# Where a decoder step makes its output weights' Strassen factors: in rooms of their own in the sample phase, one job later, some stores by ScalarE's queue

## The chip, the cores and the metric

One core of one Trainium2 chip runs the whole program. The metric is the device time of one execution in microseconds (us); the time of a kernel is the median of its runs.

## The reference, cut to what matters

One layer of a decoder is computed for 1024 prompt tokens and 64 sample tokens (1088 columns in all). Three branches (retention, causal pooling, sparse attention) are projected to the model width, gated, summed and projected once more:

```
b_a = (silu(rg) * o_a) @ w_br_a          # first branch:  (1024, D)
b_b = (silu(pg) * o_b) @ w_br_b          # second branch: (512, D)
b_c = (silu(ng) * o_c) @ w_br_c          # third branch:  (512, D)
gates = sigmoid(mg).reshape(n, t, 3, D)  # mg = rms_norm(x) @ w_in[:, 5912:]
merged = gates[:, :, 0] * b_a + gates[:, :, 1] * b_b + gates[:, :, 2] * b_c
y = rms_norm(x + merged @ w_out, final_gain)
```

Every float32 weight is split into a high and a low float16 part, and a product is three float16 matmuls. The large products (the gates, `w_br_a`, `w_out`) are made by a Strassen scheme with seven products in place of eight, so their weights are first added and subtracted by quarters and then split.

## The kernel before, in words

The program runs in phases: keys and values, prompt attention, retention, **sample phase** (pooling and the attention of the sample tokens), **output**. Within a phase the order of the instructions on each engine is set by the compiler's scheduler, from the dependences and from which buffers (rooms) are free; each engine, and each queue of DMA issues (SP's, ScalarE's, GpSimd's), works through its own list in order.

The weight pipe is a pool with rooms that all phases share: three for raw weights (`raw`, 128x1024 float32), three for high parts (`whi`) and three for low parts (`wlo`); every third one comes from a second pool (`wtile`, L212). A weight is loaded into a raw room; `wsplit` (L218) makes the high part on ScalarE (L220) and the low part on VectorE (L221).

**Sample phase.** `sample_attention` (L1020) takes the eight sequences in four groups of two. For each group SP issues two transposing DMAs of the keys (`sks<-skd`, L1041), TensorE makes the scores (L1055, L1058), VectorE and ScalarE the softmax (L1062 to L1081), TensorE transposes the weights (`ta`, `tb`, L1084 to L1087), ScalarE and VectorE split them (`sph`, `spl`, L1091 to L1094), TensorE multiplies them with the values (`so`, L1103, L1106) and transposes the sum (`sto`, L1112). The pooling branch fills TensorE beside this: its projections (`pj`, L307 to L309) and its small products (`y`, L1461) end in `gb`, the second branch's input. At its end `out_weights` (L1496) prepares `w_out` in four jobs: a job loads two row blocks of `w_out`, splits them and stores the parts to DRAM (`wod`), makes four differences on VectorE (L1517), and splits and stores these too (`wtd`). That is two loads, four splits, four differences and eight stores a job; rooms from the weight pipe, all DMAs by SP.

**Output.** For each of four pairs of column blocks the second branch's product is made: `load_c` loads and splits a pair's `w_br_b` (two halves, L231), and 96 matmuls (`pb`, L1645 to L1647) follow in eight tiles, each copied out by ScalarE (L1696). Beside each pair, `store_pair` (L1521) loads two raw rooms of `w_br_a` (L1481), has GpSimd make the Strassen sums (four operations, L1485, L1486), splits seven blocks into rooms of the weight pipe and stores them to DRAM (`wad`, L1524), all DMAs by SP. TensorE's next work is the first of eight gate jobs (`strassen`, L1551), whose left factors `load_pair` makes in the same way from `w_in`. In its first job the products "11" and "12" need raw columns only; the third, "S2", needs GpSimd's sums. The last four pairs read the stored `wad` back (`stored_pair`), and `out_rows` multiplies with `wod` and `wtd`.

Rooms that the change uses: `q` (six rooms of 128x576 float32, L1542) and `T4a` (128x4352 float16, first read in the fifth gate job).

Of the kernel before, what the change touches and what calls it, by code (L numbers as in the profile page):

```python
# [20 lines left out]
P = 128  # L21
# [106 lines left out]
class Kern:  # L128
# [32 lines left out]
    def run(self):  # L161
# [26 lines left out]
        with ExitStack() as eo:  # L188
            self.smc = self.pool(eo, "smc")
            self.pjb = R_PJ  # L190
            with ExitStack() as es:
                self.psb, ppj, psa = [self.pool(es, x, bufs=1, space=PSUM) for x in ("rpsb", "rppj", "rpsa")]
                self.retention(es, ppj, psa, right)
            self.gbp = self.pool(right, "gbp", side="right")
            self.gb = self.gbp.tile([P, 4, NG, 2, 32], F16, tag="gb", name="gb", bufs=1)
            with ExitStack() as es:
                psb, ps, pst = [self.pool(es, x, bufs=1, space=PSUM) for x in ("spsb", "sppj", "spst")]
                sp = self.pool(es, "smp", bufs=1)
                pool = self.pooling(es, ps, pst)
                next(pool)  # L200
                with self.behind():
                    self.sample_attention(sp, psb, pst)
                next(pool, None)
                self.out_weights()
# [1265 lines left out]
    def load_pair(self, wq, src, c0, c1):  # L1470
# [6 lines left out]
        for c in (c0, c1):  # L1477
# [3 lines left out]
            self.loaded = self.wq.dma_start(raw[-1].rearrange("p (k c) -> p k c", c=P),  # L1481
# [7 lines left out]
        for i, a in (("11", a11), ("12", a12), ("S2", s2), ("S1", s1), ("S3", a21), ("S4", a11), ("22", a22)):  # L1489
            if i == "S2":  # L1490
                sub(a11, a12, s2)
            t = self.wblock(wq)
# [3 lines left out]
    def out_weights(self):  # L1496

        nc = self.nc
        self.wod = self.dr.tile([P, 8, 2, 1024], F16, name="wod")

        self.wtd = self.dr.tile([P, 2, 4, 2, 1024], F16, name="wtd")

        def keep(dst, raw):
            hl = [self.wtile([P, 8, P], F16, x).rearrange("p k c -> p (k c)") for x in ("whi", "wlo")]
            self.wsplit(*hl, raw)
            for a in range(2):
                nc.sync.dma_start(dst[:, a], hl[a])

        for j in range(4):
            raw = []  # L1510
            for k in (j, j + 4):
                raw.append(self.wtile([P, 1024], F32, "raw"))
                nc.sync.dma_start(raw[-1], self.d["w_out"][0][k * P:(k + 1) * P, :])
                keep(self.wod[:, k], raw[-1])
# [6 lines left out]
    def store_pair(self, wq, i, c0, c1):  # L1521

        for n, (_, t) in enumerate(self.load_pair(wq, self.d["w_br_a"][0], c0, c1)):
            self.nc.sync.dma_start(self.wad[:, i, n], t.rearrange("p a k c -> p a (k c)"))  # L1524
# [125 lines left out]
    def output(self, es):  # L1650
# [9 lines left out]
        with ExitStack() as e:  # L1660
# [6 lines left out]
            for i, x in ((2, "T2"), (1, "T3"), (3, "T4")):  # L1667
                nc.sync.dma_start(tx[x], self.txd[:, i])
            rx = self.factors(lambda k, t, c0, n: [x[:, k, t * H + c0:t * H + c0 + n] for x in xs], 4, tx)
            t4a = room(wk, "T4a", 4)  # L1670
            jobs = [(w, C_MG + br * 1024, p) for br in (1, 2) for p in pairs]
            loads = chain((self.load_pair(wk, x, *[c + j * P for j in p]) for x, c, p in jobs),
                          (self.stored_pair(wk, i) for i in range(4)))
            self.wad = self.dr.tile([P, 4, 7, 2, 512], F16, name="wad")
# [11 lines left out]

            for p in pairs:
                wb = self.load_c(*[d["w_br_b"][0][:, j * P:j * P + P] for j in p])
                self.store_pair(wk, p[0], *[j * P for j in p])
                if p == pairs[-1]:  # L1690
                    state.update(A=dict(next(loads)), more=iter(()))
                for i, j in enumerate(p):
# [4 lines left out]
            for gi, (_, _, p) in enumerate(jobs):  # L1697
                if gi == 4:

                    x = self.gbp.tile([P, 2, 2, 4, H], F16, tag="gb", name=self.nm("ta"), bufs=1)  # L1700
                    ra, ma = self.right_sums(wk, self.by32(self.ga_at), 4, {"T2": x[:, 0], "T3": x[:, 1], "T4": t4a})
# [257 lines left out]
```

## Time and profile before

| | us |
|---|---|
| median of 3 runs (lowest, highest) | 1356.6 (1355.98, 1359.17) |
| the profiled execution's own time | 1358.71 |
| its span, first to last instruction | 1356.8 |
| TensorE busy in the span | 1257.2 (93%) |
| VectorE, ScalarE, GpSimd busy | 912.7, 629.5, 516.8 |

The page shows busy shares of 40 slices of 33.9 us each; the stretch of the change is slices 23 to 30. Times in rows are us from the span's start. In a timeline, the number in brackets is how long the engine sat idle before the instruction, and what ended that.

### The profile page before, as it was taken

To read this page: it belongs to the slowest core of one execution; us is meant where nothing else is said; L and a number is where in the kernel's file an instruction comes from. 1 tells how busy PE (TensorE), PEld (TensorE's weight loads), DVE (VectorE), ACT (ScalarE), POOL (GpSimd) and SP (SyncE) were. 2 spreads that over 40 slices of the span, in tenths; PEclk is the share of its full clock that TensorE was granted. 3 is DMA by queue.
4 is the path that set the end of the run, shared out by engine and by line. 5 is a ranking of instruction groups with operands and counts; after the bars stand their busy time and mean duration, and the time that the engine had idled before them with its cause. 6 is when DMAs were issued, how large, how long until landed. Compare 5 with 4: busy or idle time off the path is not lost. (4 is left out here: it accounts for less than half of the span.)

```text
span 1356.8 us, 27917 instructions
## 1 busy us (share of the span) xinstructions
PE 1257.2 (93%) x10520; PEld 851.8 (63%) x10520; DVE 912.7 (67%) x2280; ACT 629.5 (46%) x1466; POOL 516.8 (38%) x561
## 2 busy tenths in 40 slices
PE   7999899999998997999999999946779999999997
PEld 4556566776766663555555666625568888888644
DVE  6657536777676754675856487775669977558854
ACT  5533436667666654564644433434534434112212
POOL 1112004665766641445553531002334555323322
PEclk8999899999999999999999999968989999999999
DMA  7776624777999985334630463188643112474432
GB/s 254 166 129 148 153 63 87 119 132 152 166 173 182 172 181 152 84 96 125 166 101 23 128 133 101 61 311 281 210 119 123 48 48 56 133 246 138 153 116 86
DMA packets 330555, 187.10 MB, mean 138 GB/s; under 512 B 204785, under 2 KB 303057, under 8 KB 330004
## 3 DMA queue, kind: packets, MB, share of 16 engines
q1 hardware_dynamic: 299348, 154.35, 47.0%
q10 hardware_dynamic: 26336, 17.67, 4.7%
q0 software_dynamic: 4736, 13.31, 3.4%
q8 instruction: 82, 1.34, 0.4%
q14 instruction: 53, 0.43, 0.1%
HBM read 100.64 MB, written 39.28 MB: 103 GB/s over the span
## 5 line engine op out<-in xcount | busy, mean ns | idle before, releaser
L756 POOL TENSOR_TENSOR hl<-S,hl 128x640 f16<-128x640 f32 (+7 forms) x128 | 152.4, 1200 | 153.7 <-DVE hl L755 90.4
L307 PE MATMUL pj<-xh,whi 128*128 128x384 f16 (+1 forms) x480 | 153.2, 319 | 0.5 <-DVE gc L934 0.5
L308 PE MATMUL pj<-xl,whi 128*128 128x384 f16 (+1 forms) x480 | 153.2, 319 | 0.0
L309 PE MATMUL pj<-xh,wlo 128*128 128x384 f16 (+1 forms) x480 | 153.1, 319 | 0.0
L286 PE MATMUL z<-rwh,xh 128*128 128x512 f16 x256 | 97.5, 381 | 0.0
L287 PE MATMUL z<-rwl,xh 128*128 128x512 f16 x256 | 97.5, 381 | 0.0
L288 PE MATMUL z<-rwh,xl 128*128 128x512 f16 x256 | 97.3, 380 | 0.0
L751 ACT ACTIVATE S<-S,nm 128x640 f32<-128x640 f32 (+7 forms) x128 | 93.7, 732 | 4.0 <-DVE gc L934 0.4
L220 ACT ACTIVATE whi<-raw 128x1024 f16<-128x1024 f32 (+1 forms) x69 | 63.2, 922 | 66.8 <-PE pj L308 15.6
L1575 DVE TENSOR_TENSOR q<-st,q 128x288 f32<-128x288 f32 (+1 forms) x168 | 70.4, 434 | 32.0 <-PE st L1566 31.0
L309 PEld LDWEIGHTS <-wlo 128*128 128x128 f16 x672 | 66.0, 98 | 35.4 <-issue 1.3
L307 PEld LDWEIGHTS <-whi 128*128 128x128 f16 x672 | 66.0, 98 | 33.4 <-issue 1.2
L308 PEld LDWEIGHTS <-whi 128*128 128x128 f16 x672 | 66.0, 98 | 33.3 <-issue 2.3
L1486 POOL TENSOR_TENSOR ws<-raw 128x512 f32<-128x512 f32 x12 | 15.8, 1313 | 182.5 <-DMA raw<-w_br_a 128.5
L221 DVE SCALAR_TENSOR_TENSOR wlo<-raw,whi 128x1024 f16<-128x1024 f32 x48 | 58.5, 1221 | 27.1 <-ACT whi L220 23.0
L286 PEld LDWEIGHTS <-xh 128*128 128x128 f16 x448 | 45.4, 101 | 46.3 <-issue 7.3
L1322 PE MATMUL o<-vst,pt 128*128 128x64 f16 x528 | 57.8, 194 | 17.5 <-DMA pt<-hl 17.2
L288 PEld LDWEIGHTS <-xl 128*128 128x128 f16 x448 | 44.2, 99 | 45.8 <-issue 2.0
L287 PEld LDWEIGHTS <-xh 128*128 128x128 f16 x448 | 44.1, 98 | 43.1 <-issue 2.2
L847 DVE CUSTOM_DVE_ANT_0 S<-pn,tnear 128x256 f32<-128x256 f32 (+1 forms) x128 | 47.3, 403 | 32.9 <-PE pn L841 27.4
L1645 PE MATMUL pb<-gb,whi 128*128 128x352 f16 (+1 forms) x128 | 36.8, 295 | 33.6 <-ACT whi L220 33.6
L1322 PEld LDWEIGHTS <-pt 128*128 128x128 f16 x528 | 47.4, 98 | 27.5 <-DMA pt<-hl 24.1
(492 smaller groups left out, 4057.5 us busy)
## 6 DMA issues: line engine op xcount, KB each, us to landing
raw<-w_in SPq DMA_DIRECT2D x26, 512.0 KB
raw<-w_in ACTq DMA_DIRECT2D x18, 512.0 KB
raw<-w_in SPq DMA_DIRECT2D x48, 128.0 KB
txd<-rso SPq DMA_DIRECT2D x8, 544.0 KB
raw<-egd SPq DMA_DIRECT2D x16, 272.0 KB
s<-state_ret SPq DMA_DIRECT2D x16, 256.0 KB
o_ret_s<-s POOLq DMA_DIRECT2D x16, 256.0 KB, 2.9
raw<-w_out SPq DMA_DIRECT2D x8, 512.0 KB
```

What stands on the lines that cost most here:

```text
L220: a = nc.scalar.activation(hi, raw, AF.Copy, scale=WS)
L221: b = nc.vector.scalar_tensor_tensor(lo, raw, WS, hi, op0=ALU.mult, op1=ALU.subtract)
L286: nc.tensor.matmul(out, xh, hi[:, k, c0:c0 + n], start=(k == 0), stop=False)
L287: nc.tensor.matmul(out, xh, lo[:, k, c0:c0 + n], start=False, stop=False)
L288: self.marks["PE"] = nc.tensor.matmul(out, xl, hi[:, k, c0:c0 + n], start=False, stop=(k == 7))
L307: nc.tensor.matmul(out, hi[:, k, :], xh, start=(k == 0), stop=False)
L308: nc.tensor.matmul(out, hi[:, k, :], xl, start=False, stop=False)
L309: nc.tensor.matmul(out, lo[:, k, :], xh, start=False, stop=(k == 7))
L751: nc.scalar.activation(s[:, c0:c1], s[:, c0:c1], AF.Exp, bias=nm[:, br:br + 1], scale=0.125, accum_out=l[:, 0, br, r:r + 1])
L756: nc.gpsimd.tensor_tensor(hl[:, w:2 * w], s[:, d0:c1], hl[:, :w], op=ALU.subtract)
L1322: nc.tensor.matmul(out, lhs[0], rhs[0], start=start, stop=False)
L1575: nc.vector.tensor_tensor(out[:, c0:c0 + n], b, x[:, c0:c0 + n], op=ALU.add)
```

## The change

`out_weights` becomes a function of the jobs, the rooms and the queue. Jobs 0 to 2 are made in the sample phase in rooms of their own (two pairs of raw rooms, two for high parts, one for low parts), by SP; job 3 in the output phase beside the second branch's first pair, raw in `T4a`, parts in `q`, by ScalarE's queue. `store_pair` writes its blocks into `q` in place of the weight pipe's rooms, and loads and stores by ScalarE's queue; it now prepares pairs 1 to 3. The first pair of `w_br_a` isn't stored: it becomes a ninth job of `load_pair`, made just before its use. The second branch's `w_br_b` is loaded one pair ahead.

```diff
-                self.out_weights()
+                self.wod = self.dr.tile([P, 8, 2, 1024], F16, name="wod")
+                self.wtd = self.dr.tile([P, 2, 4, 2, 1024], F16, name="wtd")
+                wo = self.pool(es, "wout", bufs=2)
+                self.out_weights(range(3), lambda: [wo.tile([P, 1024], F32, tag="wr", name=self.nm("wr")) for _ in range(2)],
+                                 lambda: [wo.tile([P, 1024], F16, tag="w" + x, name=self.nm("w" + x), bufs=n) for x, n in (("h", 2), ("l", 1))],
+                                 self.nc.sync)
...
-            self.loaded = self.wq.dma_start(raw[-1].rearrange("p (k c) -> p k c", c=P),
+            self.loaded = (queue or self.wq).dma_start(raw[-1].rearrange("p (k c) -> p k c", c=P),
...
-            t = self.wblock(wq)
+            t = block() if block else self.wblock(wq)
...
-            hl = [self.wtile([P, 8, P], F16, x).rearrange("p k c -> p (k c)") for x in ("whi", "wlo")]
+            hl = halves()
             self.wsplit(*hl, raw)
             for a in range(2):
-                nc.sync.dma_start(dst[:, a], hl[a])
...
+                queue.dma_start(dst[:, a], hl[a])
...
-        for n, (_, t) in enumerate(self.load_pair(wq, self.d["w_br_a"][0], c0, c1)):
-            self.nc.sync.dma_start(self.wad[:, i, n], t.rearrange("p a k c -> p a (k c)"))
+        q = self.nc.scalar
+        block = lambda: self.quarter(wq)[:, :512].bitcast(F16).rearrange("p (a c) -> p a c", a=2)
+        for n, (_, t) in enumerate(self.load_pair(wq, self.d["w_br_a"][0], c0, c1, q, block)):
+            q.dma_start(self.wad[:, i, n], t.rearrange("p a k c -> p a (k c)"))
...
-            jobs = [(w, C_MG + br * 1024, p) for br in (1, 2) for p in pairs]
+            jobs = [(w, C_MG + br * 1024, p) for br in (1, 2) for p in pairs] + [(d["w_br_a"][0], 0, pairs[0])]
...
-                          (self.stored_pair(wk, i) for i in range(4)))
+                          (self.stored_pair(wk, i) for i in range(3)))
...
+            second = lambda j: self.load_c(*[d["w_br_b"][0][:, i * P:i * P + P] for i in pairs[j]])
+            nxt = second(0)
             for p in pairs:
-                wb = self.load_c(*[d["w_br_b"][0][:, j * P:j * P + P] for j in p])
-                self.store_pair(wk, p[0], *[j * P for j in p])
+                wb = nxt
+                if p < pairs[-1]:
+                    nxt = second(p[0] + 1)
+                if p == pairs[0]:
+                    x = room(wk, "T4a", 4).rearrange("p a k c -> p (a k c)").bitcast(F32)
+                    self.out_weights((3,), lambda: [x[:, o:o + 1024] for o in (0, 1024)],
+                                     lambda: [self.quarter(wk)[:, :512].bitcast(F16) for _ in range(2)], nc.scalar)
                 if p == pairs[-1]:
                     state.update(A=dict(next(loads)), more=iter(()))
+                else:
+                    self.store_pair(wk, p[0], *[j * P + P for j in p])
```

The scheduler then orders the whole anew. Three places, with each kernel's own line numbers (six more in the sample phase's lines of the changed kernel, 13 more for the copies).

TensorE, end of the sample phase: where the last group's softmax is transposed (`ta`; `pj` are the pooling branch's projections, `y` its small product). Before:

```order
L1084 MATMUL ta_12031<-ident,sS_12008 128x128 x2
L1461 MATMUL y_12678<-dd_12534,wpl 128x384
L1084 MATMUL ta_12031<-ident,sS_12008 128x128 x2
L307 LDWEIGHTS whi_12646
L307 MATMUL pj_12683<-xh,whi_12646 128x384
```

Now:

```order
L315 MATMUL pj_12716<-xh,wlo_12647 128x320
L1467 MATMUL y_12744<-dd_12534,wpl 128x320
L1118 MATMUL sto_11938<-ident,soc_11935 128x128
L1090 MATMUL ta_12031<-ident,sS_12008 128x128 x4
L1109 LDWEIGHTS sph_12039
L1109 MATMUL so_12047<-svs_11952,sph_12039 32x128
L1092 MATMUL tb_12036<-ident,sS_12008 128x128
L1093 MATMUL tb_12036<-ident,sS_12008 64x128
```

Before, 48 projections and two small products followed the last group's `ta`; now all of them stand ahead of it, and nine of them lie between that group's scores and its `ta`.

SP, sample phase: the last group's two key transposes. Before:

```order
L1513 DMA raw_12761<-w_out 128x1024
L1041 DMA_TRANSPOSE sks_11953<-skd_11954 128x8x128
L1041 DMA_TRANSPOSE sks_11953<-skd_11960 128x8x128
L1513 DMA raw_12785<-w_out 128x1024
L1507 DMA wod<-whi_12755 128x1024
```

Now:

```order
L1511 DMA wtd<-wh_12840 128x1024
L1511 DMA wtd<-wl_12841 128x1024
L1511 DMA wtd<-wh_12846 128x1024
L1511 DMA wtd<-wl_12847 128x1024
L1047 DMA_TRANSPOSE sks_11953<-skd_11954 128x8x128
L1047 DMA_TRANSPOSE sks_11953<-skd_11960 128x8x128
```

Before, all eight transposes stood ahead of the first store of `w_out`'s factors; now all 24 stores of jobs 0 to 2 stand ahead of the last two.

ScalarE, from the sample phase's last cast (`gc`) into the second branch's first pair. Before:

```order
L220 ACTIVATE whi_12869<-raw_12849 128x1024
L220 ACTIVATE whi_12875<-raw_12857 128x1024
L220 ACTIVATE whi_12911<-raw_12908 128x1024
L220 ACTIVATE blk_12924<-raw_12915 128x512
L220 ACTIVATE blk_12928<-raw_12915 128x512
L1696 COPY mm<-pb_12953 128x352
```

Now:

```order
L1126 CAST gc<-sgt 128x4x2x32
L1516 DMA T4a_12893<-w_out 128x1024 x2
L1709 COPY mm<-pb_12962 128x352
L1709 COPY mm<-pb_12976 128x192
L1709 COPY mm<-pb_12990 128x352
L226 ACTIVATE q_12895<-T4a_12893 128x1024
L1709 COPY mm<-pb_13004 128x192
L1511 DMA wod<-q_12895 128x1024
L1709 COPY mm<-pb_13018 128x352
L1511 DMA wod<-q_12896 128x1024
```

Before, the split of the first pair's `w_br_b` (`whi_12911`) stood behind the splits of `w_out`'s last jobs; now it lies far ahead of `gc`, and the copies of the first tiles follow at once, with job 3 and its stores between them.

## Rows read from the trace of the kernel before

**Rows 1.** The page's part 2: TensorE and DMA, 40 equal slices.

```profile
PE   7999899999998997999999999946779999999997
...
DMA  7776624777999985334630463188643112474432
```

**Rows 2.** Windows by stage: us, busy us of each engine, clock, DMA share, GB/s.

```profile
775.00:890.00 115.00, 114.80 (x924) 72.56 (x922) 84.90 (x237) 45.90 (x114) 17.89 (x19) 1.00 0.45 115
890.00:900.30 10.30, 5.74 (x43) 3.54 (x43) 7.68 (x14) 4.48 (x9) 0.00 (x0) 0.67 1.00 340
900.30:924.90 24.60, 0.00 (x0) 0.00 (x0) 15.59 (x22) 9.22 (x11) 0.00 (x0) 0.50 0.88 320
924.90:994.10 69.20, 53.45 (x432) 40.54 (x432) 37.79 (x39) 33.70 (x73) 27.44 (x19) 0.94 0.72 221
994.10:1340.00 345.90, 345.64 (x2846) 265.83 (x2847) 254.77 (x455) 105.10 (x208) 136.19 (x111) 0.99 0.38 116
```

**Rows 3.** TensorE's timeline from the sample phase's end: start, us, instruction, idle before.

```profile
899.86 0.45 PE L1112 MATMUL sto<-ident,soc 128*128 128x128 f32 x1 [0.70 <-DVE soc L1110]
924.94 0.47 PE L1645 MATMUL pb<-gb,whi 128*128 128x352 f16 x1 [24.64 <-ACT whi L220]
938.60 0.32 PE L1645 MATMUL pb<-gb,whi 128*128 128x352 f16 x1 [1.07 <-ACT whi L220]
953.45 0.32 PE L1645 MATMUL pb<-gb,whi 128*128 128x352 f16 x1 [3.55 <-ACT whi L220]
969.09 0.47 PE L1645 MATMUL pb<-gb,whi 128*128 128x352 f16 x1 [4.35 <-ACT whi L220]
981.63 0.29 PE L1564 MATMUL st<-xh,blk 128*128 128x288 f16 x1
994.12 0.42 PE L1564 MATMUL st<-T,wlo 128*128 128x288 f16 x1 [6.77 <-ACT wlo L220]
```

**Rows 4.** SP's and ScalarE's timelines, 900 to 955.

```profile
910.21 2.85 SPq L231 DMA_DIRECT2D raw<-w_br_b  x2
...
938.05 0.41 SPq L1481 DMA_DIRECT2D raw<-w_br_a  x1
...
923.83 1.06 ACT L220 ACTIVATE whi<-raw 128x1024 f16<-128x1024 f32 x1 [2.27 <-DMA wod<-whi]
```

**Rows 5.** GpSimd's timeline in the second branch: the Strassen sums of successive pairs.

```profile
930.50 1.26 POOL L1486 TENSOR_TENSOR ws<-raw 128x512 f32<-128x512 f32 x1 [100.60 <-DMA raw<-w_br_a]
...
934.86 1.60 POOL L1485 TENSOR_TENSOR raw<-raw,ws 128x512 f32<-128x512 f32 x1
945.36 1.27 POOL L1486 TENSOR_TENSOR ws<-raw 128x512 f32<-128x512 f32 x1 [8.90 <-DMA raw<-w_br_a]
...
990.04 1.26 POOL L1486 TENSOR_TENSOR ws<-raw 128x512 f32<-128x512 f32 x1 [7.51 <-DMA wad<-wlo]
```

**Rows 6.** VectorE's groups, 775 to 906: count, busy us, mean ns.

```profile
L221 DVE SCALAR_TENSOR_TENSOR wlo<-raw,whi 128x1024 f16<-128x1024 f32 x16 | 19.4, 1220 | 4.1 <-ACT whi L220 4.1
...
L1517 DVE TENSOR_TENSOR raw<-raw,raw 128x512 f32<-128x512 f32 x6 | 4.1, 687 | 0.0
```

**Rows 7.** The last group's softmax: scores on TensorE, last step on VectorE.

```profile
868.98 0.35 PE L1058 MATMUL s<-kcs,qsts 128*32 128x64 f16 x8
...
876.77 1.11 DVE L1081 TENSOR_SCALAR sS<-sS,sst 128x256 f32<-128x256 f32 x5
```

**Rows 8.** A window while SP's loads of one pair of `w_br_a` land (columns as above).

```profile
938.00:945.40 7.40, 6.80 (x59) 5.26 (x60) 2.73 (x4) 1.97 (x5) 0.04 (x1) 1.00 1.02 290
```

**Rows 9.** Waits, 760 to 1000 and 775 to 925: total us, times, longest.

```profile
SPq L1524 <- DVE wlo L221: 15.3, 6, 3.6
SPq L1524 <- DVE blk L221: 12.4, 9, 3.2
SPq L1524 <- DVE whi L221: 8.8, 9, 3.3
...
DVE wlo L221 <- DMA wtd<-wlo: 1.6, 1, 1.6
```

More of the change, by code (lines that the diff above doesn't have):

```diff
@@ L1467, in pool_gate, with load_pair @@
             nc.vector.tensor_tensor(self.gb[:, g, cs, 1, :], tv, self.gb[:, g, cs, 0, :], op=ALU.subtract)
-    def load_pair(self, wq, src, c0, c1):
+    def load_pair(self, wq, src, c0, c1, queue=None, block=None):
         nc = self.nc
@@ L1491, in load_pair, with out_weights @@
                 sub(a11, a12, s2)
-            t = self.wblock(wq)
+            t = block() if block else self.wblock(wq)
             self.wsplit(t[:, 0, :n], t[:, 1, :n], a)
             yield i, t[:, :, :n].rearrange("p a (k c) -> p a k c", c=P)
-    def out_weights(self):
+    def out_weights(self, js, rooms, halves, queue):
         nc = self.nc
-        self.wod = self.dr.tile([P, 8, 2, 1024], F16, name="wod")
-        self.wtd = self.dr.tile([P, 2, 4, 2, 1024], F16, name="wtd")
         def keep(dst, raw):
-            hl = [self.wtile([P, 8, P], F16, x).rearrange("p k c -> p (k c)") for x in ("whi", "wlo")]
+            hl = halves()
             self.wsplit(*hl, raw)
             for a in range(2):
-                nc.sync.dma_start(dst[:, a], hl[a])
[L1509 to L1514, printed above, removed]
+                queue.dma_start(dst[:, a], hl[a])
+        for j in js:
+            raw = rooms()
+            for k, r in zip((j, j + 4), raw):
+                queue.dma_start(r, self.d["w_out"][0][k * P:(k + 1) * P, :])
+                keep(self.wod[:, k], r)
             b11, b12, b21, b22 = [x[:, o:o + 512] for x in raw for o in (0, 512)]
@@ L1669, in output @@
             rx = self.factors(lambda k, t, c0, n: [x[:, k, t * H + c0:t * H + c0 + n] for x in xs], 4, tx)
-            t4a = room(wk, "T4a", 4)
-            jobs = [(w, C_MG + br * 1024, p) for br in (1, 2) for p in pairs]
+            jobs = [(w, C_MG + br * 1024, p) for br in (1, 2) for p in pairs] + [(d["w_br_a"][0], 0, pairs[0])]
             loads = chain((self.load_pair(wk, x, *[c + j * P for j in p]) for x, c, p in jobs),
-                          (self.stored_pair(wk, i) for i in range(4)))
-            self.wad = self.dr.tile([P, 4, 7, 2, 512], F16, name="wad")
+                          (self.stored_pair(wk, i) for i in range(3)))
+            self.wad = self.dr.tile([P, 3, 7, 2, 512], F16, name="wad")
             state = {}
@@ L1696, in output @@
                         nc.scalar.copy(acc[:, j, t, c0:c0 + n], pb)
-            for gi, (_, _, p) in enumerate(jobs):
+            for gi, (_, _, p) in enumerate(jobs[:8]):
                 if gi == 4:
                     x = self.gbp.tile([P, 2, 2, 4, H], F16, tag="gb", name=self.nm("ta"), bufs=1)
+                    t4a = room(wk, "T4a", 4)
                     ra, ma = self.right_sums(wk, self.by32(self.ga_at), 4, {"T2": x[:, 0], "T3": x[:, 1], "T4": t4a})
```

## The prediction

> **What bounds the kernel now.** I read the page's 40 slices first: TensorE is at 9 nearly everywhere, with one hole in slices 27 to 30, where the DMA engines are busiest [rows 1]. Windows by stage say how deep it is: up to 890 us TensorE is busy for 114.80 of 115.00 us, after 994 us for 345.64 of 345.90; between lie a sample-phase tail with 10.30 - 5.74 = 4.6 us idle, 24.6 us with nothing at all, and 69.2 us of which 53.45 are busy [rows 2]. So only the stretch from 890 to 994 us can give time, and new waits anywhere else cost it.
>
> TensorE's timeline names the waits. The sample phase's last instruction ends at 899.86 + 0.45 = 900.3. The second branch's four pairs then wait 24.64, 1.07, 3.55 and 4.35 us, each for ScalarE's high part of a `w_br_b`; the first gate job's third product waits 6.77 us more [rows 3]. That is 40.4 us. ScalarE and SP show why the first is long: the split at 923.83 waited for a room whose store of `w_out` parts had not landed, and SP issued the load of `w_br_b` only at 910.21, behind stores of that job [rows 4]. The remaining pairs go at GpSimd's pace: its sums start at 930.50 and 945.36, and the gate job's, the fifth, at 990.04, so a cycle takes (990.04 - 930.50) / 4 = 14.9 us, against 11.3 us that a pair takes TensorE undisturbed (938.60 to 953.45 - 3.55) [rows 3, 5].
>
> **The change, part by part.** I measure from E, the sample phase's end (900.3), to S2, the gate job's third product (994.12): 93.8 us. It is made of 40.4 us of waits, four pairs of 11.3 (45.2), 994.12 - 6.77 - 981.63 = 5.7 for two products, and 12.59 + 12.54 - 2 x 11.3 = 2.5 that the first and fourth pair lose after a wait, when TensorE starts after standing; over the 24.6 us without work the granted clock was 0.50, the lower of its two levels, 1.2 GHz [rows 2, 3]. Without waits it would be 45.2 + 5.7 = 50.9 us.
>
> *`w_out`'s jobs 0 to 2 and `w_br_b` a pair ahead.* In the order, three of the four `w_br_b` are now split ahead of the sample phase's end and share no room with `w_out`'s parts. The wait of 24.64 and the three between pairs go: -33.6 us, with the clock loss -36.1. What is late next is the gate job's S2.
>
> *S2.* `w_br_a`'s two raw rooms are still reused: a pair's sums must end before the next load. Before, a cycle of 14.9 us is 7.3 us from the issue at 938.05 to the sums, 934.86 + 1.60 - 930.50 = 6.0 of sums, and 1.6 until the room is free and SP issues [rows 4, 5]. Now one of the two columns is loaded earlier, into another room, so the first sum (1.26 us) leaves the cycle and a load has half the bytes in flight. The bounds are 14.9 and 10 us (6.0 and 1.6 with a load of 2.4, 0.52 MB at the 221 GB/s of this stretch [rows 2]); nothing says which is nearer, so I take the middle, 12.5. Pair 1's raw is loaded in the sample phase, but ScalarE splits it behind job 3 of `w_out`, whose raw (1.05 MB) is issued at E beside three loads of Strassen sums (3.3 MB). If the two queues share the 340 GB/s of the tail [rows 2], its MB lands after 2 x 1.05 MB, 6.2 us, and I add 3 us for issue and landing: E + 9 (an estimate). With four splits and four differences after that (4 x 1.22 + 4 x 0.69 = 7.6 us [rows 6]) pair 1's splits begin at E + 17 and its room is free at E + 23. That is a cycle whose sums began at E + 15.5, since from first sum to next issue is 938.05 - 930.50 = 7.5. Three cycles of 12.5 lead to E + 53, and from the gate job's sums to S2 it is 994.12 - 990.04 = 4.1: S2 at E + 57. TensorE is there at E + 51 and **waits 6 us**, as before. Bounds: 0, and 13 with cycles of 14.9.
>
> *ScalarE.* It gains 29 stores, 6 raw loads and job 3's loads. They stand behind copies and splits that give VectorE its time; an issue took SP 0.41 us [rows 4]. I take nothing, hidden by eight PSUM banks: copies may be eight tiles late (11.3 us) before TensorE stops. If that cover goes, see rival 3.
>
> *The sample phase.* VectorE must do 20 wide splits and 12 differences where it did 15 and 10: 5 x 1.22 + 2 x 0.69 = 7.5 us more, in 30.1 us of idle [rows 2, 6]: nothing. The reordered tail costs: from the last group's scores (868.98) to its scaled softmax took 876.77 + 1.11 - 869.3 = 8.6 us, under 56 projections in the order [rows 7]. Now nine lie there, some 1.2 us, with a `y` and a `sto`, so TensorE stands 6 to 7 us; the steps to `sto` after it (splits of `ta` and `tb`, 3 us exposed) replace the 4.6 us idle of the tail before. I take **+6 us**, bounds 0 (if TensorE comes late to the scores anyway) and 12 (the chain twice as exposed). Everything behind S2 is as before: GpSimd and VectorE have the room for the ninth `load_pair` (136 and 255 of 346 us busy [rows 2]).
>
> **Sum.** S2 moves from E + 93.8 to E + 57: -37; E moves by +6: **-31 us**. The profiled execution took 1358.71 us, 2.1 above the median of 1356.6; 1356.6 - 31 gives **1326 us** (bounds of this case 1314 to 1339).
>
> **Rivals.**
> 1. *All of it* (S2 waits for nothing, the tail hides): -43, **1314**. For it: loads of 512 KB alone are shorter than three together. Against: the tail's new order leaves nine projections.
> 2. *Loads stay as slow as they are.* While one pair's `w_br_a` lands, the DMA share is 1.02 [rows 8], and the bytes of that stretch hardly fall. Then a cycle stays at 14.9, S2 comes at E + 15.5 + 3 x 14.9 + 4.1 = E + 64, 13 us late: -24, **1333**. The Trainium skill, "Trainium Kernel Development and Optimization", under Key Constraints, says that DMAs from the SP, ACT and POOL queues run on the same 16 DMA engines, so several queues save only issue time; by that rule ScalarE's queue shortens no load, which is this rival, and the share of 1.02 agrees.
> 3. *ScalarE is the new bound.* Stores wait in its own list for VectorE's low part; SP's waits for that were 15.3 + 12.4 + 8.8 = 36.5 us in 24 [rows 9], 1.5 each. If 29 stores cost ScalarE that in full, 44 us stand on top of its own 33.70 for this stretch [rows 2]: S2 at E + 75 to 78 in place of 57, **1345**. Against: the order puts two or three other instructions between a split and its store.
> 4. *Slower: one room for `wl`.* VectorE's low part waits until the store before has landed, and SP's list mixes those stores with key transposes that wait for TensorE. If each of 11 reuses holds VectorE for s, TensorE loses 11 s less the 22.6 us still idle (30.1 - 7.5). It decides from s = 5.2 us, where the -37 are eaten with the tail (11 x 5.2 - 22.6 = 35); at 6.5 us the loss is 49 and the time **1375**. Against: the longest such wait in the rows is 1.6 us, with three rooms [rows 9].
> 5. *The change doesn't do what it says:* `w_br_b` still late, since SP's list has it behind stores of `w_out`. The order has the splits early, so I give this no case of its own; it would look like rival 3.
>
> **How the numbers follow.** Forecast (1318 to 1334) 0.55; rival 1 0.15; rival 2 0.15; rival 3 0.09; rival 4 0.06. What differs from no change by under 0.3% (4 us) can't be told from it. The first four cases are faster by more, but for 0.01 at rival 3's far end: 0.55 + 0.15 + 0.15 + 0.08 = 0.93. Rival 4 has 0.05 slower and 0.01 within, so same is 0.02. The range takes in rival 1 and rival 2 and the forecast's bounds: **1311 to 1341**.
>
> **What would show it.** In the changed profile: `pb`'s first matmul follows `sto` with under 2 us idle; no waits for `whi` between pairs; one wait of about 6 us at `st` before S2; GpSimd's sums 12 to 13 us apart; `ta` of the last group waiting 6 to 7 us for VectorE; TensorE full before and after. The prediction is wrong if TensorE stands in the middle of the sample phase (rival 4), or stands at `pb` for a copy on ScalarE (rival 3).

## The result and the profile after

The changed kernel takes 1341.2 us (median of 4 runs, 1338.51 to 1346.42), the kernel before 1357.88 us beside it; the ratio is 0.988, its 95% interval 0.984 to 0.992. That is 16.7 us less, where 31 were forecast, and 0.2 us outside the range. The execution that was profiled is the longest of the four (1346.42 us, span 1344.6), so its own sum is 1346.42 - 1358.71 = -12.3 us. By TensorE's timeline it falls into these pieces:

| piece | before | forecast | after |
|---|---|---|---|
| first `ptb` (before 781.64, after 783.77) to E, the sample phase | 118.7 | +6 | 131.3 (+12.6) |
| E to S2 | 93.8 | 57 | 65.6 (-28.2) |
| S2 to the end of the span | 362.7 | as before | 363.9 (+1.2) |

The remaining +2.1 us lie ahead of the first `ptb`, where the change moves nothing; over all kernels below that instant lies anywhere from 777.5 to 783.9 us.

The page of the changed kernel, busy tenths in 40 slices of TensorE, of its granted clock and of the DMA engines:

```profile
PE   6899899999998998999999999989789999999997
...
PEclk9999899999999999999999989998889999999998
DMA  7866624678889896243730396535642122364432
```

The hole of [rows 1] is nearly closed; what is left of it stands at slice 27 (from 874 us) and slices 29 and 30 (941 to 1008 us), counted from 1 as in the prediction. TensorE's timeline says what they are; first the sample phase (columns as in [rows 3]):

```profile
799.69 0.40 PE L1061 MATMUL s<-sks,qsts 128*32 128x256 f16 x2 [3.21 <-DMA sks<-skd]
...
854.29 0.32 PE L313 MATMUL pj<-xh,whi 128*128 128x384 f16 x1 [2.45 <-ACT ue L1423]
...
905.66 1.09 PE L1090 MATMUL ta<-ident,sS 128*128 128x128 f32 x4 [4.82 <-DVE sS L1087]
907.42 0.29 PE L1109 MATMUL so<-svs,sph 128*32 128x128 f16 x1 [0.68 <-ACT sph L1097]
908.15 0.48 PE L1092 MATMUL tb<-ident,sS 128*128 128x128 f32 x1 [0.44 <-DVE spl L1098]
...
914.61 0.44 PE L1118 MATMUL sto<-ident,soc 128*128 128x128 f32 x1 [0.71 <-DVE soc L1116]
914.85 0.50 PE L1650 MATMUL pb<-gb,whi 128*128 128x352 f16 x1
```

and then the output stage:

```profile
951.99 0.32 PE L1652 MATMUL pb<-gb,wlo 128*128 128x352 f16 x1 [1.43 <-DVE wlo L227]
966.04 0.42 PE L1569 MATMUL st<-xh,blk 128*128 128x288 f16 x1 [3.06 <-ACT blk L226]
969.44 0.42 PE L1571 MATMUL st<-xh,blk 128*128 128x288 f16 x1 [2.74 <-DVE blk L227]
...
980.67 0.42 PE L1569 MATMUL st<-T,blk 128*128 128x288 f16 x1 [4.17 <-ACT blk L226]
```

`pb` follows `sto` at once: the 24.64 us of [rows 3] are gone, and of the waits between the pairs 1.43 is left. At the last group's `ta` TensorE waits 4.82 us, where 6 to 7 were forecast; the whole tail's wait is 4.82 + 0.68 + 0.44 + 0.71 = 6.65 us, against 4.6 us before [rows 2]. Not forecast are the waits inside the sample phase (3.21 and 2.45, with TensorE at a granted clock of 0.86 between 800 and 820 us, after the first of them) and three waits instead of one ahead of S2. The whole phase, before and after (columns as in [rows 2]):

```profile
781.64:900.30 118.66, 113.89 (x922) 71.59 (x920) 90.10 (x243) 47.65 (x116) 15.60 (x17) 0.97 0.49 134
```

```profile
783.77:915.05 131.28, 118.17 (x923) 73.25 (x922) 101.08 (x256) 55.14 (x123) 22.71 (x20) 0.93 0.61 173
```

TensorE stands 13.1 us in place of 4.8 and is busy 4.3 us longer with as many matmuls, at a granted clock of 0.93 in place of 0.97. VectorE is busy 11.0 us longer, and its idle time is 30.2 us in place of 28.6: none of it was used. The 2.45 us come by way of ScalarE: its copy `ue`, which TensorE waited for, stood behind the issue of a `w_br_a` load in its own list, and that waited for VectorE's low part:

```profile
853.32 0.39 ACTq L1487 DMA_DIRECT2D raw<-w_br_a  x1
853.75 0.49 ACT L1423 ACTIVATE ue<-pj 128x384 f32<-128x384 f32 x1 [2.50 <-DVE wlo L227]
```

GpSimd's Strassen sums, which answer to [rows 5]: the third and the fourth of pair 1, the first and the fourth of the gate job:

```profile
872.68 1.72 POOL L1491 TENSOR_TENSOR raw<-raw,raw 128x512 f32<-128x512 f32 x1
...
934.21 1.59 POOL L1491 TENSOR_TENSOR raw<-raw,ws 128x512 f32<-128x512 f32 x1 [59.82 <-DVE q L227]
...
976.38 1.27 POOL L1492 TENSOR_TENSOR ws<-raw 128x512 f32<-128x512 f32 x1 [8.74 <-DMA raw<-w_in]
...
981.06 1.60 POOL L1491 TENSOR_TENSOR raw<-raw,ws 128x512 f32<-128x512 f32 x1
```

Pair 1's first three sums were made in the sample phase (870 to 874 us); the one at E + 19.2 is its last. So a cycle is taken here from last sum to last sum: three of them lie between 934.21 and 981.06, 15.6 us each. Before, the gate job's last sum stood at

```profile
994.90 1.62 POOL L1485 TENSOR_TENSOR raw<-raw,ws 128x512 f32<-128x512 f32 x1
```

and four cycles from 934.86 [rows 5] took 15.0 us each. ScalarE's timeline shows what stood ahead of pair 1's splits, the parts of `w_out`'s job 3, and, in pair 3, a load behind a store that was not ready:

```profile
921.56 1.06 ACT L226 ACTIVATE q<-T4a 128x1024 f16<-128x1024 f32 x1
...
931.03 1.06 ACT L226 ACTIVATE q<-T4a 128x1024 f16<-128x1024 f32 x1 [0.17 <-issue]
...
932.71 1.15 ACT L226 ACTIVATE q<-raw 128x512 f16<-128x512 f32 x2
...
939.62 0.48 ACTq L1487 DMA_DIRECT2D raw<-w_br_a  x1
...
951.96 0.39 ACTq L1487 DMA_DIRECT2D raw<-w_br_a  x1
...
953.17 2.82 ACTq L1529 DMA_DIRECT2D wad<-q  x1
956.02 0.46 ACTq L1487 DMA_DIRECT2D raw<-w_br_a  x1
```

### The profile page after: what moved, and what is told of

The parts are those of the page before. It is cut to its first block, busy times and chain, and to the rows that moved or that the text cites. A ratio compares the mean times of both kernels' runs of the same rounds, so it can differ in the third digit from the quotient of the medians.

```text
span 1344.6 us, 27854 instructions
## 1 busy us (share of the span) xinstructions
PE 1262.1 (94%) x10520; PEld 853.8 (63%) x10520; DVE 910.8 (68%) x2280; ACT 631.8 (47%) x1466; POOL 521.1 (39%) x561
## 5 line engine op out<-in xcount | busy, mean ns | idle before, releaser
L1580 DVE TENSOR_TENSOR q<-st,q 128x256 f32<-128x256 f32 (+1 forms) x168 | 70.3, 433 | 27.7 <-PE st L1571 26.9
L226 ACT ACTIVATE whi<-raw 128x1024 f16<-128x1024 f32 (+1 forms) x48 | 45.4, 946 | 69.2 <-PE pj L314 16.4
L1260 POOL TENSOR_TENSOR rh<-rot,rh 128x256 f16<-128x256 f32 (+1 forms) x36 | 26.0, 721 | 96.1 <-ACT rh L1259 95.8
L315 PE MATMUL eg<-xh,wlo 128*128 128x384 f16 (+1 forms) x192 | 62.0, 323 | 0.0
L314 PE MATMUL eg<-xl,whi 128*128 128x384 f16 (+1 forms) x192 | 62.0, 323 | 0.0
```

Of the source, the lines that this page charges most:

```text
L226: a = nc.scalar.activation(hi, raw, AF.Copy, scale=WS)
L314: nc.tensor.matmul(out, hi[:, k, :], xl, start=False, stop=False)
L315: nc.tensor.matmul(out, lo[:, k, :], xh, start=False, stop=(k == 7))
L1580: nc.vector.tensor_tensor(out[:, c0:c0 + n], b, x[:, c0:c0 + n], op=ALU.add)
```

## The experiments

Theory 1: two parts of the change give back what it saves: the jobs in the sample phase, by standing in VectorE's list between the steps of the four groups of scores, and job 3, by standing ahead of `w_br_a`'s splits. The rivals are transfers and queues. All kernels that do the whole work first, then those that leave some out; lengths are taken as in the table above, each from the one execution that was profiled; the times are medians of 4 runs, which lie 2 to 8 us apart, beside runs of the kernel before (medians 1357.9 to 1360.5).

| kernel | phase | E to S2 | S2 to end | time | ratio to before |
|---|---|---|---|---|---|
| changed kernel | 131.3 | 65.6 | 363.9 | 1341.2 | 0.988 |
| all four jobs in the sample phase | 130.0 | 52.3 | 361.7 | 1326.3 | 0.976 |
| all four in the gate jobs | 113.7 | 58.0 | 378.3 | 1332.3 | 0.980 |
| all four, on GpSimd | 137.8 | 57.0 | 363.3 | 1339.2 | 0.984 |
| all four, low parts on GpSimd | 139.5 | 54.1 | 363.0 | 1341.3 | 0.986 |
| `w_br_a`'s loads by SP | 125.6 | 63.2 | 364.6 | 1339.6 | 0.985 |
| jobs behind the first group's keys | 129.0 | 63.2 | 365.0 | 1338.6 | 0.984 |
| two jobs there, two in pairs 2 and 3 | 123.2 | 52.7 | 362.4 | 1322.7 | 0.972 |
| one there, three in pairs 2 to 4 | 123.1 | 56.3 | 379.4 | 1342.5 | 0.986 |
| without jobs 0 to 2 | 113.3 | 69.8 | 361.4 | 1327.4 | 0.976 |
| without job 3 | 131.4 | 53.0 | 361.8 | 1327.9 | 0.976 |
| all four, without VectorE's part | 118.5 | 57.0 | 363.7 | 1326.1 | 0.975 |
| without jobs 0 to 2's transfers | 128.3 | 67.2 | 364.5 | 1341.7 | 0.987 |

**Without jobs 0 to 2.**

```diff
-                self.out_weights(range(3), lambda: [wo.tile(
+                self.out_weights(range(0), lambda: [wo.tile(
...
```

> Left out: w_out's jobs 0 to 2 (their loads, splits, differences and stores); the last product reads job 3's parts in their place. It prices these jobs in the sample phase, whose length from the first ptb to the end of its last sto was 118.7 us before and 131.3 us in the changed kernel. Theory 1, the jobs are what lengthens it, by their places in VectorE's and SP's lists and in the order of the projections: the length comes back to between 113 and 119 us (118.7 less some of the 4.6 us that the tail stood before), E to S2 stays near 65.6 us, and the time is 13 to 18 us under the changed kernel's, 1323 to 1328. Rival, the four early loads and splits of w_br_b and the early raw of w_br_a lengthen it: it stays at 127 us or more, and the time over 1336.

The phase fell by 18.0 us to 113.3, and the time to 1327.4: theory 1. E to S2 did not stay: it grew from 65.6 to 69.8 us, so 4 us of the gain came back there.

**Without job 3.**

```diff
...
-                    self.out_weights((3,), lambda: [x[:, o:o + 1024] for o in (0, 1024)],
-                                     lambda: [self.quarter(wk)[:, :512].bitcast(F16) for _ in range(2)], nc.scalar)
...
```

> Left out: w_out's job 3 (in the first pair of the output stage); the last product reads job 0's parts in its place. It prices job 3 between E (end of the last sto) and S2 (third product of the first gate job), 65.6 us in the changed kernel. Theory 1, job 3's four splits and eight stores stand ahead of w_br_a's first splits in ScalarE's list and start its cycle of rooms late (first sum at E + 19.2, S2 46.5 us after it): without it the first sum comes at E + 3 to 6, S2 at E + 51 to 54, the time 11 to 15 us under the changed kernel's, 1326 to 1330. Rival, w_br_a's loads set the pace by themselves, in rooms and transfers that do not depend on job 3: S2 at E + 60 or later, and the time at most 5 us lower, 1336 or more.

GpSimd's sums without job 3, the last of pair 1 and of the gate job, and S2 on TensorE:

```profile
915.86 1.59 POOL L1491 TENSOR_TENSOR raw<-raw,ws 128x512 f32<-128x512 f32 x1 [43.18 <-issue]
...
963.56 1.60 POOL L1491 TENSOR_TENSOR raw<-raw,ws 128x512 f32<-128x512 f32 x1
```

```profile
966.21 0.28 PE L1569 MATMUL st<-T,blk 128*128 128x288 f16 x1 [0.43 <-ACT mm L1705]
```

With E at 913.20 pair 1's last sum, the expectation's "first sum", comes at E + 2.7 in place of E + 19.2, S2 comes at E + 53.0 and waits for no load: job 3 costs 12.6 us in this place, as theory 1 said. The cycle stays: (963.56 - 915.86) / 3 = 15.9 us.

**All four jobs in the sample phase.**

```diff
-                self.out_weights(range(3), lambda: [wo.tile(
+                self.out_weights(range(4), lambda: [wo.tile(
...
-                    self.out_weights((3,), lambda: [x[:, o:o + 1024] for o in (0, 1024)],
-                                     lambda: [self.quarter(wk)[:, :512].bitcast(F16) for _ in range(2)], nc.scalar)
```

> All four jobs of w_out in the sample phase, none in the first pair; all work is done. Theory 1: E to S2 as without job 3, 51 to 54 us, and the sample phase longer by a fourth job's share of what three cost (12.6 / 3 = 4 us): 135 us. Sum -12 + 4: 1331 to 1335. Rival, job 3 was not what held S2: E to S2 60 us or more, and the time 1340 to 1346.

E to S2 fell to 52.3 us as expected. But the fourth job cost the phase nothing (130.0), so its length does not go by the job, and the time, 1326.3, is better than expected.

**All four in the gate jobs.**

Besides these lines, the two places of the changed kernel's jobs are emptied:

```diff
...
+                if gi < 4:
+                    x = room(wk, "T4a", 4).rearrange("p a k c -> p (a k c)").bitcast(F32)
+                    self.out_weights((gi,), lambda: [x[:, o:o + 1024] for o in (0, 1024)],
+                                     lambda: [self.quarter(wk)[:, :512].bitcast(F16) for _ in range(2)], nc.sync)
```

> All four jobs of w_out moved behind the second branch, one to each of the first four gate jobs, in the room of T4a, which is free until the fifth; by SP's queue. All work is done. Theory 1: the sample phase comes back to 113 to 119 us, E to S2 comes to 51 to 56 us, and the gate jobs, in which TensorE was busy all the time and VectorE some 74% of it, hide the jobs: 1341 - 13 to 18 - 9 to 14, so 1310 to 1319. Rival, VectorE or ScalarE becomes late for TensorE's products in the gate jobs: S2 to the end grows from 363.9 us by 10 us or more, and the time is 1322 or more.

The phase came down to 113.7 us, but the rival was right about the rest: S2 to the end took 378.3 us, 14.4 more, mostly in waits of TensorE for VectorE, of which these are two:

```profile
976.36 0.28 PE L1569 MATMUL st<-xh,whi 128*128 128x288 f16 x1 [1.01 <-DVE q L1580]
982.15 0.27 PE L1569 MATMUL st<-T,blk 128*128 128x256 f16 x1 [1.37 <-DVE q L1580]
```

**All four, on GpSimd.** To take the work off VectorE's list, ScalarE scales each raw once, and GpSimd makes differences and low parts.

```diff
...
-            self.wsplit(*hl, raw)
+            nc.scalar.copy(hl[0], raw)
+            nc.gpsimd.tensor_tensor(hl[1], raw, hl[0], op=ALU.subtract)
...
                 queue.dma_start(r, self.d["w_out"][0][k * P:(k + 1) * P, :])
+                nc.scalar.activation(r, r, AF.Copy, scale=WS)
...
-                nc.vector.tensor_tensor(o, x, y, op=ALU.subtract)
+                nc.gpsimd.tensor_tensor(o, x, y, op=ALU.subtract)
...
```

> All four jobs of w_out in the sample phase, but nothing of them on VectorE: ScalarE scales each raw by 64 in place (one more instruction for each raw, eight in all), GpSimd makes the 16 low parts and the 16 differences. All work is done; loads and stores stay on SP's queue. Theory 1, the jobs lengthen the sample phase by their places in VectorE's list, where each step of the four groups of scores waits behind them until the projections are used up: first sto back from 62 to 65 us after ptb to 44 to 47, the phase back from 130 to 113 to 119 us, E to S2 51 to 54 us, time 1326 less 11 to 17, so 1309 to 1316. Rival, it is the jobs' loads and stores, on SP's list and the DMA engines: the phase stays at 126 us or more, and the time is 1322 or more; GpSimd's work holding back its gathers, or VectorE, would look the same and show as waits for them.

**All four, low parts on GpSimd.** The same without the last two lines of that diff.

> As with all four jobs on GpSimd and ScalarE, but the 16 differences stay on VectorE (16 of 0.68 us, 10.9 us). Theory 1: between the two, the phase 119 to 126 us, the time 1315 to 1322. Rival, transfers and SP's list: as all four jobs in the sample phase, 128 us or more, and 1324 to 1329.

Both missed: 137.8 and 139.5 us, longer than with everything on VectorE. The work had left VectorE, but its busy time had not fallen: 112.5 us of the phase's 137.8 with the jobs on GpSimd, against 108.3 of 130.0 with all four on VectorE. VectorE's groups by line and shape (count, busy us, mean ns of one) say why. With the jobs on VectorE:

```profile
L1468 DVE SCALAR_TENSOR_TENSOR th<-y,psc,th 128x384 f32<-128x384 f32 x8 | 4.9, 611 | 1.3 <-PE y L1467 1.2
L1046 DVE TENSOR_TENSOR svs<-sraw,svs 128x512 f16<-128x512 f32 x6 | 4.1, 682 | 0.0
L1445 DVE TENSOR_TENSOR win<-win 128x1037 f32<-128x1037 f32 x3 | 3.7, 1231 | 0.0
L1431 DVE COPY tl<-us 128x120 f32<-128x120 f32 x4 | 0.8, 209 | 0.0
```

With the jobs on GpSimd:

```profile
L1046 DVE TENSOR_TENSOR svs<-sraw,svs 128x512 f16<-128x512 f32 x6 | 7.8, 1330 | 0.0
L1445 DVE TENSOR_TENSOR win<-win 128x1037 f32<-128x1037 f32 x3 | 7.3, 2425 | 0.0
L1468 DVE SCALAR_TENSOR_TENSOR th<-y,psc,th 128x384 f32<-128x384 f32 x6 | 3.7, 609 | 0.2 <-PE y L1467 0.2
L1431 DVE COPY tl<-us 128x120 f32<-128x120 f32 x4 | 3.0, 744 | 0.0
```

These additions and copies from SBUF took about twice as long, the smallest 3.6 times; L1468, which reads one input from PSUM, took what it took (611 and 609 ns). The Trainium skill, "SBUF — State Buffer", "SBUF: two separate sides", states a rule that these rows agree with: VectorE, in a fast mode or, against a GpSimd operation that reads SBUF, with two SBUF inputs, and GpSimd lock one pair of ports for a whole instruction, and the other waits. So this kernel does not tell the theories apart: it took the work off the list and put a wait in its place.

**All four, without VectorE's part.** This does.

```diff
...
-            self.wsplit(*hl, raw)
+            nc.scalar.activation(hl[0], raw, AF.Copy, scale=WS)
...
-                queue.dma_start(dst[:, a], hl[a])
+                queue.dma_start(dst[:, a], hl[0])
...
-            for o, x, y in ((b11, b12, b11), (b12, b22, b12), (b22, b22, b11), (b21, b21, b22)):
-                nc.vector.tensor_tensor(o, x, y, op=ALU.subtract)
...
```

> All four jobs in the sample phase with their loads, ScalarE's high parts and all stores, but VectorE's work of them left out: the 16 low parts (the high part is stored twice in their place) and the 16 differences. Theory 1, VectorE's list lengthens the sample phase: as without the jobs, 113 to 119 us from ptb to E; with E to S2 of 51 to 58 us the time is 1308 to 1316. Rival, the jobs' transfers, SP's list and ScalarE's copies lengthen it: 124 us or more, and 1320 or more.

**Without jobs 0 to 2's transfers.** And the other way round:

```diff
-                queue.dma_start(dst[:, a], hl[a])
+                if 3 in js:
+                    queue.dma_start(dst[:, a], hl[a])
...
-            raw = rooms()
+            if j == js[0]:
+                raw = rooms()
...
-                queue.dma_start(r, self.d["w_out"][0][k * P:(k + 1) * P, :])
+                if j == js[0]:
+                    queue.dma_start(r, self.d["w_out"][0][k * P:(k + 1) * P, :])
...
```

> The changed kernel with the stores of jobs 0 to 2 left out, and their loads but for the first two; VectorE's and ScalarE's work on them stays, on the same two rooms (the last product reads job 3's parts). Job 3 stays in the first pair. Theory 1, VectorE's list: the phase keeps 124 us or more of the changed kernel's 125.6 to 131.4, and the time stays over 1334. Rival, transfers and SP's list: 113 to 119 us, and 1323 to 1330.

The phase took 118.5 us without VectorE's part and 128.3 us without the transfers: both by theory 1. The last group's `ta` started 98.0 us behind `ptb` without jobs 0 to 2, 103.2 without VectorE's part, 118.2 without the transfers and 121.9 in the changed kernel. Without stores SP's list can't wait for low parts either, so that is not what lengthens the phase. Windows of the phase, columns as in [rows 2]. Without VectorE's part:

```profile
800.00:820.00 20.00, 20.00 (x124) 12.05 (x121) 15.62 (x46) 9.94 (x21) 0.00 (x0) 0.89 0.87 270
820.00:840.00 20.00, 20.00 (x189) 13.07 (x189) 11.69 (x42) 13.32 (x29) 5.52 (x6) 1.00 1.01 296
```

Without the transfers:

```profile
800.00:820.00 20.00, 17.86 (x113) 11.37 (x111) 18.59 (x44) 9.22 (x21) 0.00 (x0) 1.00 0.26 67
820.00:840.00 20.00, 18.81 (x167) 11.20 (x166) 20.00 (x47) 10.15 (x16) 0.00 (x0) 1.00 0.24 53
```

With the DMA engines full (0.87 and 1.01) and VectorE at 12 to 16 of 20 us, TensorE works without a gap; with the DMA engines at a quarter and VectorE at 19 to 20 of 20, it stands for 1 to 2 us. Just ahead of these windows, at 798.65, the first of the two kernels had its one long wait, 3.33 us for `sks`; the second had none. So this wait came with the transfers. What they cost is bounded by 118.5 - 113.3 = 5.2 us. The time of the first of the two, 1326.1, missed its 1308 to 1316 and is no better than that of the kernel with all four jobs (1326.3): its E to S2 was 57.0 in place of the 52.3 of the kernel with all four jobs, in waits for ScalarE's copies of `pb`, its profiled phase began at 783.0 us in place of 778.4, and S2 to the end took 363.7 in place of 361.7.

**Jobs behind the first group's keys.** The first visible delay in the changed kernel is a job's low part between two steps of the first group. VectorE's timeline after:

```profile
787.68 1.22 DVE L227 SCALAR_TENSOR_TENSOR wl<-wr,wh 128x1024 f16<-128x1024 f32 x1
788.81 1.23 DVE L1445 TENSOR_TENSOR win<-win 128x1037 f32<-128x1037 f32 x1
789.96 0.68 DVE L1046 TENSOR_TENSOR skd<-sraw,skd 128x512 f16<-128x512 f32 x1
```

That last operation began 6.2 us behind `ptb`; in the kernel before it began at 785.54, 3.9 us behind. To see whether this one delay carries the rest:

```diff
...
-                nc.sync.dma_start_transpose(ks[:, b], kd.rearrange("p q g a c -> p (q g a c)"))
+                z = nc.sync.dma_start_transpose(ks[:, b], kd.rearrange("p q g a c -> p (q g a c)"))
+                if tt == 0 and b == 1:
+                    self.late = z
...
+                with self.tc.issue_after(self.late.ins):
+                    self.out_weights(range(3), lambda: [wo.tile(
...
```

> The changed kernel with jobs 0 to 2 put behind the first group's key transposes in SP's list (their VectorE and ScalarE work follows). Theory 1, it is the sum of the jobs' work in VectorE's list: the first wait for sks falls under 1.5 us, but the phase stays at 126 to 131 us and the time at 1336 to 1342. Rival, it is the first group's keys, late by 4.4 us and followed by a slow clock, that hold back the first sto (65.5 us after ptb against 44.0 without the jobs) and all after it: the first sto comes at 50 us or earlier, the phase at 120 us or less, the time at 1328 to 1331.

The wait for `sks` fell to 0.89 us, the phase stayed at 129.0 us, the first `sto` came 68.8 us after `ptb` (846.27 - 777.48): theory 1. It is not one step of the list. The 2.45 us by way of ScalarE were gone too, and TensorE waited 2.18 and 2.20 us for other steps of VectorE instead.

Nor is it the sum of the work, which the expectation named. The kernel before has nine splits and nine differences of `w_out` on VectorE in this phase (17 us; the kernel with two jobs below has eight and eight, 15 us), but all of them behind the last group's keys:

```profile
840.06 0.69 DVE L1040 TENSOR_TENSOR skd<-sraw,skd 128x512 f16<-128x512 f32 x1 [1.07 <-ACT skd L1039]
...
857.79 1.23 DVE L221 SCALAR_TENSOR_TENSOR wlo<-raw,whi 128x1024 f16<-128x1024 f32 x1 [1.68 <-ACT whi L220]
```

Its last `ta` started 98.1 us behind `ptb`, as without jobs, and its phase took 118.7 us, where the one with two jobs takes 123.2. The two kernels differ in more than this, but it is the place in the list that they bear out, not the amount.

**`w_br_a`'s loads by SP.**

```diff
-        for n, (_, t) in enumerate(self.load_pair(wq, self.d["w_br_a"][0], c0, c1, q, block)):
+        for n, (_, t) in enumerate(self.load_pair(wq, self.d["w_br_a"][0], c0, c1, self.nc.sync, block)):
```

> The changed kernel with w_br_a's loads on SP's queue; its stores stay on ScalarE's. In the three other kernels so far the sums of w_br_a came 13.7 to 14.4 us apart, as in the changed kernel (14.06) and nearly as before (14.9). Theory 1, that pace is the rooms and the transfer, whatever queue issues: still 13.5 to 14.5 us, E to S2 64 to 66 us, the time 1339 to 1343. Rival, loads stand behind stores in ScalarE's list (in the changed kernel a pair's second load went out at 956.02, behind a store of 2.82 us, 4.1 us after the first): the pace falls to 12.5 to 13, S2 comes 3 to 5 us earlier, the time is 1336 to 1338.

The expectation counts from pair 1's last sum to the gate job's first (14.06 us a cycle in the changed kernel). So counted, the sums came (965.71 - 925.69) / 3 = 13.34 us apart, 0.7 less than there and just under theory 1's bound; from last sum to last sum it is (970.39 - 925.69) / 3 = 14.9 us, again 0.7 less. S2 came 2.4 us earlier, the time was 1339.6. So the queue has a small share (0.7 us of a cycle), and the rest stays with transfers and rooms, which no run separates. Windows while loads were in flight, pair 2's and pair 3's:

```profile
930.80:936.10 5.30, 5.30 (x48) 4.12 (x47) 0.52 (x1) 1.03 (x3) 0.00 (x0) 1.00 0.98 294
943.80:952.40 8.60, 8.54 (x74) 6.65 (x75) 1.20 (x2) 1.32 (x5) 1.27 (x1) 1.00 0.92 268
```

The DMA engines are taken for 0.98 and 0.92 of that time. The Trainium skill, "Trainium Kernel Development and Optimization", "Key Constraints", says that DMAs of several queues share the same engines and save only issue time; by that rule little was to be won, and the run agrees. This kernel's sample phase took 125.6 us, with the jobs of the changed kernel and without job 3 in the same places (131.3 and 131.4) but for two loads: its wait for `sks` was 0.61 us in place of 3.21, and the wait by way of ScalarE was gone, since the load no longer stood in ScalarE's list. The wait for `sks` does not go by the number of jobs: with all four of them it was 0.99 us.

**Two jobs in the sample phase, two in pairs 2 and 3**, behind `store_pair` in program order, by SP's queue.

```diff
...
-                self.out_weights(range(3), lambda: [wo.tile(
+                self.out_weights(range(2), lambda: [wo.tile(
...
                     self.store_pair(wk, p[0], *[j * P + P for j in p])
+                if p[0] in (1, 2):
+                    x = room(wk, "T4a", 4).rearrange("p a k c -> p (a k c)").bitcast(F32)
+                    self.out_weights((p[0] + 1,), lambda: [x[:, o:o + 1024] for o in (0, 1024)],
+                                     lambda: [self.quarter(wk)[:, :512].bitcast(F16) for _ in range(2)], nc.sync)
```

> Two jobs in the sample phase, one each in the second and third pair of the output stage, behind that pair's splits of w_br_a in program order and on SP's queue. All work is done. By theory 1 the sample phase takes 122 to 126 us (VectorE has half of the 30 us of four jobs to do there), VectorE has 24 of 53 us free between E and S2 for the other 15 us, S2 comes at E + 53 to 58, and the time is 1320 to 1326. Rival: as in the changed kernel, whatever is put between E and S2 delays the splits of w_br_a: S2 at E + 62 or later, and the time over 1330.

The phase and the time came as theory 1 said (123.2 and 1322.7 us), E to S2 0.3 us under its range (52.7). It is the fastest kernel of this study by its median: 0.972 of before (0.969 to 0.976), clear of the changed kernel's 0.984 to 0.992, though not of the 0.973 to 0.979 of all four jobs in the sample phase.

**One there, three in pairs 2 to 4**: the same with `range(1)`, `(1, 2, 3)` and `(p[0],)`.

> One job in the sample phase, one each in the second to fourth pair of the output stage, on SP's queue. All work is done. By theory 1 the sample phase takes 117 to 122 us and S2 comes at E + 55 to 62 (23 us of work in 24 us that VectorE has free): 1318 to 1326. Rival: the work between E and S2 delays the splits, S2 at E + 65 or later: over 1328.

The phase was no shorter than with two jobs (123.1, expected 117 to 122), S2 came at E + 56.3 as expected, and the time was 1342.5 all the same, by neither side's reason: TensorE stood behind S2, in the first gate job:

```profile
985.15 0.40 PE L1569 MATMUL st<-T,whi 128*128 128x288 f16 x1 [12.82 <-ACT q L1584]
```

SP and ScalarE at that place:

```profile
960.46 9.00 SPq L1511 DMA_DIRECT2D wtd<-q  x4
969.51 0.92 SPq L1516 DMA_DIRECT2D T4a<-w_out  x2
```

```profile
973.97 1.06 ACT L226 ACTIVATE q<-T4a 128x1024 f16<-128x1024 f32 x1 [7.31 <-issue]
...
980.97 1.15 ACT L226 ACTIVATE blk<-ws 128x512 f16<-128x512 f32 x2
```

The last job's raw could only be loaded at 969.51, behind the stores of the job before it in the one room; its splits stood in ScalarE's list ahead of the gate job's and held them for 7.31 us and more. That is the change's old stall, a list in order behind a reused room, in a new place.

## Why the prediction was wrong

*What held.* The waits of 24.64 us and most of those between the pairs went, and `pb` followed `sto`. Pair 1's splits were forecast at E + 17 and came at 932.71 - 915.05 = E + 17.7, in part by luck: job 3's raw was there for its first split at E + 6.5, not E + 9, and its work took 11.2 us, not 7.6. Everything behind S2 stayed (+1.2).

*The step that failed most.* "VectorE must do 7.5 us more, in 30.1 us of idle: nothing." The work was there (VectorE was busy 11.0 us longer), the cover was not: the idle time stayed whole. It is an engine's sum; what counted was that each group of scores goes through VectorE several times, one step after the other, and that each step now waited in its list behind splits and differences, so that the last group's `ta` started 121.9 us behind `ptb` in place of 98.1. With no job in the phase it took 113.3 us, with VectorE's part alone left out 118.5, with one or two jobs 123, with three or four 125.6 to 131.4; with the transfers gone it still took 128.3. The prediction's +6 was the tail alone: 6 to 7 us at `ta` and 3 behind it, in place of 4.6. The tail's waits were 4.82 and 1.83, 2.1 us more than before. The other 10.5 us by which the phase grew are waits ahead of the tail, above all the 3.21 and 2.45, and TensorE's 4.3 us of longer busy time; the prediction had put all of this at nothing, the 2.45 by its "I take nothing" for loads in ScalarE's list. Rival 4 had the place (TensorE standing in the sample phase) but another mechanism: VectorE waited for the single room of `wl` only 1.6 + 0.3 us, over the whole phase.

*The second step* is the cycle of the rooms. S2 at E + 57 was a room free for pair 2's load at E + 23, the gate job's sums 30 us later (three cycles of 12.5 less 7.5), and 4.1 us more. The load was issued at 939.62, E + 24.6; the gate job's sums began at 976.38, 36.8 us later; S2 came after another 4.3: 1.6 + 6.8 + 0.2 = 8.6 us late, at E + 65.6. So the start was nearly right and the pace was not: the middle between 10 and 14.9 was the wrong choice, and the cycle was no shorter than before (15.6 us from last sum to last sum, 15.0 before, and 14.9 or more in every kernel of the table). While a pair's loads were in flight the DMA engines were taken for 0.92 and 0.98 of the time, against 1.02 before [rows 8]; that they hold the cycle is not shown. Rival 2 had this nearly right (14.9, S2 at E + 64); it missed the time because it shared the first step's error. Rival 3 did not come: no `pb` waited for a copy in the changed kernel.

*What the prediction did not ask* is whether the start of that cycle was a given. It had job 3's parts ahead of pair 1's splits and took E + 17 from there; without job 3 in that place S2 came at E + 53.0. So of the 43 us of waits and clock at stake, 12.6 went to job 3's place, and in the profiled execution another 12.6 to the sample phase, of which 6 were foreseen, though in another place.

*Open:* why one job in the sample phase costs as much as two, and four as much as three. The order of the projections changes with each, and no run held that order fixed. Nor was it tried to hold the jobs, in their own rooms, back until the last group's keys are made, as they stood before. And what sets the cycle of 15 us, the transfers or the rooms, no run here shows.

## To carry to other kernels

An engine's idle time covers added work only if nothing that others wait for stands behind that work in its list: look for chains that pass the engine several times before costing anything at nothing. Where a cycle of rooms sets the pace, ask first what starts it, and put work that nobody waits for behind that start, in program order and in queue. And after moving work off a busy engine, see whether its busy time has fallen: here GpSimd took the work, and VectorE's own operations grew by as much.

## What was not expected of the hardware

GpSimd's 32 operations (groups with means of 1.6 to 2.2 us) made some of VectorE's own slower and others not (`win<-ue` of 128x1039 took 1227 and 1228 ns): `win<-win` of 128x1037 from 1231 to 2425 ns, a copy of 128x120 from 209 to 744 ns, while `th<-y,psc,th`, with an input from PSUM, stayed as it was. A page that shows VectorE as busy can mean that it stands and waits for GpSimd. And a wait of TensorE can cost more than its length: after waits for `sks` of 3.21, 3.27 and 3.33 us (changed kernel, without job 3, without VectorE's part) the granted clock was 0.86 to 0.90 over the stretch from 800 to 820 us, which is 2 to 3 us of it; after waits of 0.61 and 0.99 us (loads by SP, all four jobs in the sample phase) it was 1.00. But the length of one wait does not tell it: with the jobs on GpSimd, waits of 2.51 and 2.82 us lie in that stretch, and after the 2.45 us at 854 in the changed kernel TensorE worked on; the clock was 1.00 in both cases.
